# Which up-projection chunks of a ConvFFN go by seven products, and how their low parts are made

## The chip, the cores and the metric

The kernel runs on one core of a Trainium2 chip. The metric is the device time of the core in microseconds, the median of a few executions. An execution's trace tells, engine by engine, what ran when. The engines are TensorE (PE, with its weight loads shown apart as PEld), VectorE (DVE), ScalarE (ACT), GpSimd (POOL) and SyncE (SP); POOL and SP here mostly issue DMAs.

## The reference

Two layers of a decoder trunk over x of 512 tokens by 1024 features: layer 0 with dilated window attention, layer 1 with forgetting attention over shared keys and values, each followed by the same gated ConvFFN. The change touches the up-projection of that ConvFFN alone:

```python
D_MODEL = 1024; SEQ = 512; D_FF = 2816; CONV_W = 3

def conv_ffn(xn, w_up, cw, cb, w_down):
    a = xn @ w_up                                  # 512 x 1024 by 1024 x 5632
    T = a.shape[1]
    ap = jnp.pad(a, ((0, 0), (CONV_W - 1, 0), (0, 0)))
    a = sum(ap[:, j:j + T] * cw[j] for j in range(CONV_W)) + cb
    gate, val = jnp.split(a, 2, axis=-1)
    return (jax.nn.gelu(gate, approximate=True) * val) @ w_down
...
f = conv_ffn(rms_norm(h, g[2]), w_up[l], conv_w[l], conv_b[l], w_down[l])
h = h + rms_norm(f, g[3])
```

## The kernel before

All matrix products are exact to nearly float32 by splitting: each operand is a rounded "high" part (fp32r) plus a "low" part, the rest. A product is three matmuls, high x high, high x low and low x high; `mm3` issues them at L283, L284 and L285, whichever product it is. So every weight tile of 128 x 1024 comes into SBUF (`wraw`, loaded by SP at L50), then its high part is copied by ACT, and its low part is made in one of two ways:

- plainly: DVE subtracts the high part from the raw weight (L78 in `Weights.low`, L683 in `sub_low`);
- by an adding transfer: ACT copies the raw weight with its sign changed to the place of the low part (L71 in `Weights.minus`, L679 in `add_low`), and POOL issues a DMA that adds, so that the place ends as the difference (L98, L680). In the kernel's layout this spares DVE a pass of 128 x 1024 and costs ACT one and POOL a DMA issue.

The up-projection's 5632 columns go by 22 chunks of 128 gate and 128 value columns (`NF` = 22). The loop `for c in range(2, NF)` of `ffn` computes chunks in order; the work of the other engines is written in between by hand, since the kernel runs with a manual schedule: instructions of an engine run in the order in which the code issues them.

A *plain* chunk is two products with all 1024 features and 512 tokens (`up`): 2 x 8 x 3 = 48 matmuls of 512 columns. A chunk in `SEVEN` takes Strassen's scheme in Winograd's form on a 2 x 2 split (features by halves, tokens by halves, the two column groups as the other side): seven products named by their weights A11, S3, S2, A22, A12, S1 and S4, each of 4 x 3 matmuls of 256 columns, 84 in all. The inputs' sums (`XA`, `XB`) are made once per layer, the weights' sums per chunk by DVE (L706, L707, L709, L726), and the outputs' sums by DVE on PSUM (L963 to L1007) with a copy by ACT (L961, or L993 where the chunk was begun early).

The order within a seven chunk c that was begun early is: S2, the taps of chunk c - 1 (the convolution: ACT L620, DVE L621 and L623, then GELU L641), A22, A12, S1; then the beginning of chunk c + 1 (A11 and S3 if it is a seven, with copy L993; half of its first product if it is plain); then S4 of chunk c, and the sums of the outputs (L1001, L1007).

Weights are prepared ahead by two generators that the loop steps through with `next(steps)`: at chunk c they are chained as below, three steps are taken before the beginning of c + 1 when that is a seven, and `run` takes all that is left only under a condition:

```python
steps = chain(steps, weights_b(c + 1), weights_a(c + 2))
...
if c + 1 not in SEVEN or c + 2 in SEVEN:
    run(steps)
```

`weights_a(c)` makes the high and low parts of A11 | A12 (from the raw tile) and S3 | S2 (from the sum `sa`), in two steps; `weights_b(c)` makes S1 | S4 (from `sb`) and A22. For a plain chunk `weights_a` prepares its two tiles, one a step; `ADDED` names the chunks whose first, and whose second tile takes an adding transfer. Before, `SEVEN` has five pairs (4, 5), (7, 8), (10, 11), (13, 14), (16, 17) and the single 19. In a pair the first chunk's lows are added by transfers, the second's are made plainly; the last of them, S1 | S4's, is put off by `late` until after the sum at L1001.

## Time and profile before

| | |
|---|---|
| median of 3 executions | 1109.83 us (1109.48 to 1110.65) |
| the profiled execution | 1109.52 us, span 1107.7 us |
| granted clock of TensorE | 0.998 |
| PE busy | 1098.7 us (99%), 6609 matmuls |
| DVE busy | 876.4 us (79%) |
| ACT busy | 674.2 us (61%) |
| POOL busy | 210.0 us (19%) |
| adding transfers `w<-wsum`, `w<-wraw` | 24 and 32, of 512 KB |

Busy time is the time in which an engine executes; a share under 100% is idle or waiting. The matmuls are pipelined: the distance between the starts of two is shorter than the duration that a row shows. In a row of the timeline stand start, duration, engine, line, operation, tiles (out<-in) and, in brackets, how long the engine had been idle and what ended that. For an issue of a DMA on POOL the duration is that of the issue; when the data have landed is told by the DMA view.

### The profile page before, as it was taken

The page shows a single profiled execution, that of the slowest core. Times are in us where ns is not written, and L with a number is a line of the kernel's source. Part 1 is how long each engine was busy: PE and PEld are TensorE (multiplying, and loading weights), DVE is VectorE, ACT ScalarE, POOL GpSimd, SP SyncE. Part 2 cuts the span into 40 slices and gives each one's busy share as a digit, 9 for nine tenths or more (in the row PEclk, how much of TensorE's full clock was granted, in tenths as well). Part 3 has the DMA queues.
Part 4 walks back from the last instruction along what each step waited for, and adds up shares of the span by engine and source line. Part 5 has one row for each costly group of instructions (what it writes and reads, how often), then busy time and mean ns, then how long its engine had stood idle before and what let it go on. Part 6 is the DMA issues. An engine that isn't in the chain of part 4 may idle for free.

```text
span 1107.7 us, 18081 instructions
## 1 busy us (share of the span) xinstructions
PE 1098.7 (99%) x6609; PEld 951.8 (86%) x6609; DVE 876.4 (79%) x1493; ACT 674.2 (61%) x1116; POOL 210.0 (19%) x309
## 2 busy tenths in 40 slices
PE   9999999999999999999999999999999999999997
PEld 6988889899999988888888788789999999988886
DVE  6697788888778689997685676868887788779894
ACT  7654565755666656576451587746656666747572
POOL 2532001311111211000001445400411111211000
PEclk9999999999999999999999999999999999999999
DMA  9799854467887979793448435594368878989862
GB/s 324 171 381 412 310 161 134 98 181 190 207 199 185 245 263 328 268 333 103 152 134 301 156 96 127 163 285 121 84 178 208 197 186 189 231 266 324 314 247 76
DMA packets 184928, 236.26 MB, mean 213 GB/s; under 512 B 12352, under 2 KB 132152, under 8 KB 184840
## 3 DMA queue, kind: packets, MB, share of 16 engines
q1 hardware_dynamic: 169224, 182.94, 51.0%
q0 software_dynamic: 14944, 52.18, 20.7%
q8 instruction: 52, 0.85, 0.3%
q14 instruction: 36, 0.29, 0.1%
q10 hardware_dynamic: 672, 0.00, 0.0%
HBM read 166.08 MB, written 39.63 MB: 186 GB/s over the span
## 4 chain that ended last, share of the span: by engine, by line
PE 96%; DVE 1%; ACT 1%; issue 1%; POOL 1%; DMA 0%; DVEq 0%; SPq 0%; POOLq 0%; ACTq 0%
PE up L284 13%; PE up L283 13%; PE up L285 13%; PE acc L283 8%; PE acc L284 8%; PE acc L285 8%; PE v_ps L283 2%; PE v_ps L285 2%; PE v_ps L284 2%; PE qk_ps L284 2%; PE qk_ps L283 2%; PE qk_ps L285 2%; PE q_ps L283 1%; PE first L285 1%; PE first L283 1%; PE first L284 1%
## 5 line engine op out<-in xcount | busy, mean ns | idle before, releaser
L283 PE MATMUL acc<-w 128*128 128x512 f32 (+1 forms) x311 | 120.6, 388 | 0.3 <-DVE mix L332 0.3
L285 PE MATMUL acc<-w 128*128 128x512 f32 (+1 forms) x311 | 120.4, 387 | 0.0
L284 PE MATMUL acc<-w 128*128 128x512 f32 (+1 forms) x267 | 103.2, 387 | 0.0
L78 DVE TENSOR_TENSOR w<-wraw,w 128x1024 fp32r<-128x1024 f32 x62 | 82.3, 1347 | 22.9 <-ACT w L60 22.5
L283 PE MATMUL up<-xsh,w 128*128 128x256 f32 x352 | 99.6, 283 | 0.0
L284 PE MATMUL up<-xsl,w 128*128 128x256 f32 x352 | 99.6, 283 | 0.0
L285 PE MATMUL up<-xsh,w 128*128 128x256 f32 x352 | 99.6, 283 | 0.0
L60 ACT CAST w<-wraw 128x1024 fp32r<-128x1024 f32 x82 | 84.7, 1051 | 18.7 <-PE v_ps L284 6.9
L620 ACT ACTIVATE bb<-up,conv 128x512 f32<-128x512 f32 x80 | 59.8, 778 | 58.3 <-DVE up L1007 47.6
L284 PE MATMUL up<-xcl,w 128*128 128x512 f32 (+1 forms) x276 | 93.5, 339 | 0.0
L284 PE MATMUL up<-xbl,w 128*128 128x512 f32 (+1 forms) x276 | 93.5, 339 | 0.0
L283 PE MATMUL up<-xbh,w 128*128 128x512 f32 (+1 forms) x276 | 93.5, 339 | 0.0
L283 PE MATMUL up<-xch,w 128*128 128x512 f32 (+1 forms) x276 | 93.5, 339 | 0.0
L285 PE MATMUL up<-xbh,w 128*128 128x512 f32 (+1 forms) x276 | 93.4, 338 | 0.0
L285 PE MATMUL up<-xch,w 128*128 128x512 f32 (+1 forms) x276 | 93.4, 338 | 0.0
L283 PEld LDWEIGHTS acc<-w 128*128 128x128 f32 x311 | 58.4, 188 | 12.6 <-DVE mix L332 0.7
L285 PEld LDWEIGHTS acc<-w 128*128 128x128 f32 x311 | 58.4, 188 | 11.9
L283 PEld LDWEIGHTS up<-xsh,w 128*128 128x128 f32 x352 | 67.6, 192 | 0.0
L284 PEld LDWEIGHTS up<-xsl,w 128*128 128x128 f32 x352 | 67.6, 192 | 0.0
L285 PEld LDWEIGHTS up<-xsh,w 128*128 128x128 f32 x352 | 67.6, 192 | 0.0
L621 DVE SCALAR_TENSOR_TENSOR bb<-up,conv,bb 128x511 f32<-128x511 f32 x80 | 59.5, 744 | 6.2 <-ACT bb L620 6.1
L623 DVE SCALAR_TENSOR_TENSOR bb<-up,conv,bb 128x510 f32<-128x510 f32 x80 | 59.9, 749 | 2.8
(312 smaller groups left out, 3151.8 us busy)
## 6 DMA issues: line engine op xcount, KB each, us to landing
wraw<-in_w_up_dram SPq DMA_DIRECT2D x88, 512.0 KB, 5.4
w<-wraw POOLq DMA_DIRECT2D x32, 512.0 KB, 6.4
dT<-dsums SPq DMA_DIRECT2D x28, 512.0 KB, 7.0
w<-wsum POOLq DMA_DIRECT2D x24, 512.0 KB, 5.7
dsums<-in_w_down_dram SPq DMA_DIRECT2D x22, 512.0 KB, 7.6
dsums<-in_w_down_dram SPq DMA_DIRECT2D x44, 256.0 KB, 7.8
hD<-hc POOLq DMA_DIRECT2D x44, 256.0 KB, 6.9
dact<-hD SPq DMA_DIRECT2D x44, 256.0 KB, 5.6
```

Source lines behind the costliest of these rows:

```text
L60: self.nc.scalar.copy(pair[:, 0], raw)
L78: self.nc.vector.tensor_tensor(pair[:, 1], raw, pair[:, 0].bitcast(F32), ALU.subtract)
L283: pe.matmul(o, ah, bh, start=first, stop=False, skip_group_check=shared)
L284: pe.matmul(o, ah, bl, start=False, stop=False, skip_group_check=shared)
L285: pe.matmul(o, al, bh, start=False, stop=last, skip_group_check=shared)
L620: act.activation(bb[:, s, :], ps, AF.Identity, bias=cp[:, 3, ch:ch + 1], scale=cp[:, 2, ch:ch + 1])
L621: dve.scalar_tensor_tensor(bb[:, s, 1:], ps[:, :T - 1], cp[:, 1, ch:ch + 1], bb[:, s, 1:], ALU.mult, ALU.add)
L623: dve.scalar_tensor_tensor(bb[:, s, 2:], ps[:, :T - 2], cp[:, 0, ch:ch + 1], bb[:, s, 2:], ALU.mult, ALU.add)
```

## The change

`SEVEN` becomes four runs of three chunks, (4, 5, 6), (8, 9, 10), (12, 13, 14) and (16, 17, 18): 12 of 22 per layer in the place of 11. The plain chunks from 2 on are then 2, 3, 7, 11, 15, 19, 20 and 21. Which seven chunks get plain lows is no longer "the one behind another seven" but a list, `PLAIN_LOWS`: the middle ones 5, 9, 13 and 17. The first and the third of a run have their lows added by transfers. `ADDED` is moved to the plain chunks that are left. Since a third chunk puts nothing into `late`, the loop asks whether there is something in it. Line numbers in the changed kernel are one higher from there on, two higher behind the loop's `late`.

```diff
-SEVEN = 4, 5, 7, 8, 10, 11, 13, 14, 16, 17, 19
-
-ADDED = (6, 9, 12, 15, 18), (18, 20)
+SEVEN = 4, 5, 6, 8, 9, 10, 12, 13, 14, 16, 17, 18
+PLAIN_LOWS = 5, 9, 13, 17
+
+ADDED = (7, 11, 15, 19), (19, 20)
...
             act.copy(w[0][:, 0], r0)
-            if c - 1 not in SEVEN:
+            if c not in PLAIN_LOWS:
                 add_low(w[0], r0)
...
             dve.tensor_tensor(sa[:, 512:1024], sb[:, 0:512], a11, ALU.subtract)
-            if c - 1 not in SEVEN:
+            if c not in PLAIN_LOWS:
                 act.copy(w[1][:, 0], sa)
                 add_low(w[1], sa)
...
             (w0, w1), r0, a12, a22, sa, sb = rest.pop(c)
-            if c - 1 in SEVEN:
+            if c in PLAIN_LOWS:
                 act.copy(w1[:, 0], sa)
                 sub_low(w0, r0)
...
             act.copy(w[1][:, 0, 0:512], a22)
-            if c - 1 in SEVEN:
+            if c in PLAIN_LOWS:
                 sub_low(w1, sa)
             yield
             act.copy(w[0][:, 0], sb)
-            if c - 1 in SEVEN:
+            if c in PLAIN_LOWS:
                 late.append(lambda: sub_low(w[0], sb))
             else:
                 add_low(w[0], sb)
...
                 if c + 1 in SEVEN:
-                    late.pop()()
+                    if late:
+                        late.pop()()
                     dve.tensor_tensor(begun[2], b3, begun[1], ALU.add)
```

In the run 4, 5, 6 the third chunk's `weights_a(6)` is chained at chunk 4, behind `weights_b(5)`: its first step is the third one taken there, and its second step falls to `run` at the end of chunk 4. `weights_b(6)` and `weights_a(7)` follow at chunk 5. The two layers hold 24 chunks of seven products instead of 22.

## The prediction

> **What bounds the kernel now.** I read the page first: the slices of the span, then the chain that ended last.

> ```profile
> span 1107.7 us, 18081 instructions
> PE   9999999999999999999999999999999999999997
> PE 96%; DVE 1%; ACT 1%; issue 1%; POOL 1%; DMA 0%; DVEq 0%; SPq 0%; POOLq 0%; ACTq 0%
> ```

> TensorE (PE) is full in every slice and carries 96% of the chain. Next came the list of what PE waited for, here its two longest entries after the warm-up, and the busy time of the stage that the change touches, the first layer's up-projections (226 to 411 us):

> ```profile
> PE qk_ps L283 <- ACT w L64: 0.4, 1, 0.4
> PE pT_ps L1664 <- DVE prob L1652: 0.4, 1, 0.4
> ...
> 226.00:411.00 185.00, 185.00 (x1245) 171.71 (x1244) 146.60 (x228) 114.30 (x146) 30.60 (x43) 1.00 0.83 207
> ```

> The columns after the stretch are its length and the busy time of PE, weight loads, DVE, ACT and POOL. No wait on an `up` tile is listed, and PE is busy 185.00 of 185 us: today's preparation of weights is hidden altogether. DVE has 38 us free, ACT 71. So fewer matmuls shorten the time directly, and every new wait of PE lengthens it directly. The profiled execution took 1109.52 us, 0.31 below the median of 1109.83; I add differences to the median.

> **What PE saves.** The timeline of PE, and two rows of the same ACT copy one period apart (two chunks by seven products and a plain one):

> ```profile
> 268.12 0.28 PE L283 MATMUL up<-xsh,w 128*128 128x256 f32 x1
> 268.24 0.28 PE L284 MATMUL up<-xsl,w 128*128 128x256 f32 x1
> ...
> 278.06 0.40 PE L283 MATMUL up<-xbh,w 128*128 128x512 f32 x1
> 278.29 0.40 PE L284 MATMUL up<-xbl,w 128*128 128x512 f32 x1
> ...
> 265.44 0.37 ACT L993 COPY csum<-up 128x256 f32<-128x256 f32 x1 [0.22 <-PE up L285]
> 296.52 0.37 ACT L993 COPY csum<-up 128x256 f32<-128x256 f32 x1 [0.22 <-PE up L285]
> ```

> 256 columns take 0.12 us, so a seven chunk (7 x 4 x 3 = 84 matmuls) takes 10.08 us. The period is 31.08 us, which leaves 10.92 for a plain chunk (48 matmuls of 512 columns, 0.2275 each). The change makes one more chunk of each layer a seven (12 for 11): 2 x 0.84 = 1.7 us saved. [...] A difference under 0.2% (2.2 us) can't be told from none, so the saving alone would pass as no change.

> **Where the third chunk's weights come from.** In a run 4, 5, 6 the part `weights_a(6)` is prepared during chunk 4, its second half at the very end: the sum at L709 stands behind L1007, which needs chunk 4's last matmul. Before, a chunk whose lows are added by transfer always had a whole chunk between preparation and use. I follow the new chain from the start of chunk 5's first matmul (t = 0; in the rows 268.12), with distances between rows of before:

> ```profile
> 268.32 0.43 DVE L1007 TENSOR_TENSOR up<-up,csum 128x256 f32<-128x256 f32 x1 [0.94 <-PE up L285]
> 268.66 0.68 DVE L638 TENSOR_TENSOR hc<-bb 128x512 f32<-128x512 f32 x1
> ...
> 275.65 0.68 DVE L709 TENSOR_TENSOR wsum<-wsum,wraw 128x512 f32<-128x512 f32 x1
> ...
> 276.43 1.05 ACT L711 CAST w<-wsum 128x1024 fp32r<-128x1024 f32 x1 [2.17 <-DVE wsum L709]
> 277.38 1.05 ACT L679 ACTIVATE w<-wsum 128x1024 fp32r<-128x1024 f32 x1
> 278.73 1.46 ACT L620 ACTIVATE bb<-up,conv 128x512 f32<-128x512 f32 x2 [0.29 <-DVE up L1007]
> ...
> 278.73 0.86 POOL L680 DMA_DIRECT2D w<-wsum  x1 [3.33 <-DVE up L1007]
> ...
> w<-wsum POOLq DMA_DIRECT2D x24, 512.0 KB, 5.7
> ...
> w<-wsum POOLq DMA_DIRECT2D x1, 512.0 KB, 5.0
> ```

> L1007 starts at 0.20; the instruction behind it 0.34 later, so L709 at 0.54; L711 0.78 later, 1.32; the sign copy L679 0.95 later, 2.27; the adding transfer is issued 1.35 later, 3.62, and lands 5.7 later (median of 24), 9.3. PE wants this low part at the third matmul of chunk 6's S3, begun inside chunk 5 behind S2, A22, A12, S1 and A11: 60 x 0.12 + 0.24 = 7.44. **First wait: 1.9 us.** Bounds of the landing are 5.0 and 6.4 (the issue at 285.46, the last row, and the page's median for transfers from `wraw`, below): 1.2 to 2.6.

> A second chain holds PE nearly as long, so a quicker landing helps little. The same two ACT copies now stand ahead of chunk 4's taps (L620), and so push everything behind them:

> ```profile
> 279.55 0.75 DVE L621 SCALAR_TENSOR_TENSOR bb<-up,conv,bb 128x511 f32<-128x511 f32 x1 [0.26 <-ACT bb L620]
> 282.44 0.68 DVE L726 TENSOR_TENSOR wsum<-wraw,wsum 128x512 f32<-128x512 f32 x1
> ...
> 283.16 1.06 ACT L731 CAST w<-wsum 128x1024 fp32r<-128x1024 f32 x1 [1.35 <-DVE wsum L726]
> 284.12 1.05 ACT L679 ACTIVATE w<-wsum 128x1024 fp32r<-128x1024 f32 x1
> ...
> 263.22 1.05 ACT L60 CAST w<-wraw 128x1024 fp32r<-128x1024 f32 x1
> 264.16 1.06 ACT L71 ACTIVATE w<-wraw 128x1024 fp32r<-128x1024 f32 x1
> ```

> L620 follows L679 by 0.95: 3.22. L621 0.82 later, 4.04; L726 2.89 later, 6.93; L731 0.72 later, 7.65. Then ACT has, 0.95 apart, L679 (8.61, new here: chunk 6's S1 is low-added), L60 (9.56), L71 (10.5), and only then the copy L993 of chunk 6's first product (11.45, 0.37 long). In the built order chunk 6's first S2 matmul waits for that copy: 11.8 against 10.08 on PE, a wait of 1.75 if the first has not already cost it. The two overlap, so together 1.9; lower end 1.75.

> **The plain chunk behind the run.** L71 is the sign copy for chunk 7's first weight, whose low part L98 adds. Its landings, page first, then single issues at 265.5, 296.6, 358.8 and, L680's own, 274.6 us; min, median and maximum of all of POOL's transfers into `w`:

> ```profile
> w<-wraw POOLq DMA_DIRECT2D x32, 512.0 KB, 6.4
> ...
> w<-wraw POOLq DMA_DIRECT2D x1, 512.0 KB, 7.8
> ...
> w<-wraw POOLq DMA_DIRECT2D x1, 512.0 KB, 7.5
> ...
> w<-wraw POOLq DMA_DIRECT2D x1, 512.0 KB, 8.4
> ...
> w<-wraw POOLq DMA_DIRECT2D x1, 512.0 KB, 8.1
> ...
> DMA to landing us min/median/max: 4.5/6.1/8.8
> ...
> 265.51 0.85 POOL L98 DMA_DIRECT2D w<-wraw  x1 [9.70 <-ACT w L71]
> ...
> 274.35 0.39 PE L285 MATMUL up<-xbh,w 128*128 128x512 f32 x1
> ...
> 293.37 2.09 SPq L50 DMA_DIRECT2D wraw<-in_w_up_dram  x3
> ```

> Before, 8.84 us lay between this issue (265.51) and the matmul that needs it (274.35), and 7.5 to 8.4 of them were used: three loads of 512 KB are issued just ahead of it (last row). Now the issue comes at 10.5 + 1.35 = 11.85. Chunk 6 starts at 10.08 + 1.9 = 11.98, its four products take 48 x 0.12 = 5.76, and the low part is wanted at the third 512-column matmul, 0.46 later: 18.2. The window has shrunk to 6.35. At 7.8 us, the middle of three landings in the same place with the same loads ahead, plus now another adding transfer, **the second wait is 1.45 us**; 6.4 gives nothing, 8.4 gives 2.05.

> **What else moves, at nothing.**

> ```profile
> 262.26 1.05 ACT L731 CAST w<-wsum 128x1024 fp32r<-128x1024 f32 x1 [2.42 <-DVE wsum L726]
> ```

> The third chunk's first low part (A11) is issued 8.6 us ahead of its use (L731 stands 4.22 into a first chunk, 262.26 less 258.04; then L703 0.96, L679 0.94 and POOL 1.35 later by the distances above: 7.47 into chunk 4; wanted at 10.08 + 5.76 + 0.24 = 16.08); the 6.4 of the page fits, 8.1 still would. S1's low part is issued at 8.61 + 1.35 = 9.96 and wanted at 11.98 + 4.56 = 16.54; the `wsum` median of 5.7 fits, only because PE is already 1.9 late; without that it would wait about 1. The middle chunk keeps its lows on DVE, in the place they had. ACT gains five sign copies per layer (30 adding transfers for 25) and about three other copies, some 9 us of 71 free; DVE gains at most 6 of 38 free; POOL five issues at 0.86, and only its hidden writes of `hD` queue behind them. SP's loads keep their number.

> **Sum.** Four runs in each of two layers: 8 x (1.9 + 1.45) = 26.8, less 1.7: +25.1, that is 1134.9 us.

> **The rivals.**
> - Only the first wait: the stall lets the loads run dry, L98 lands within 6.4 like the page's median. 8 x 1.9 - 1.7 = +13.5, 1123.3 us. For it: half of all `wraw` transfers are that quick. Against: all of those in this place took 7.5 or more. Chance 0.2.
> - Transfers are quick altogether: landing in under 3.8 us (7.44 - 3.62) would end both waits on them; the copy L993 alone would hold PE 1.75: 8 x 1.75 - 1.7 = +12.3, 1122.1 us. Against it: 5.0 above, and 4.5 for the quickest of all. Chance 0.04. [...]
> - The transfers crowd each other: seven adding transfers in four chunks, for four in three, stretch L98 to 8.8, the slowest of all before. PE without waits reaches its use at 16.3, so both waits together are 11.85 + 8.8 - 16.3 = 4.35: 8 x 4.35 - 1.7 = +33, 1143 us. Chance 0.13.
> - No wait at all, because L709 gets ahead of L1007 or the lead is longer than I read from the order: -1.7, 1108.1 us, no measurable change. It decides from a chain under 7.44 where I count 9.3. Chance 0.05.
> - Faster: no waits, and the 256-column matmuls of the longer runs come at 0.11 instead of 0.12, as the second below does, the first after a stretch of 512 columns:

> ```profile
> 276.63 0.28 PE L283 MATMUL up<-xbh,w 128*128 128x256 f32 x1
> 276.74 0.28 PE L284 MATMUL up<-xbl,w 128*128 128x256 f32 x1
> ```

>   Over the 24 x 84 matmuls of both layers that is 20 us off, besides the 1.7: 1088 us. It decides only if both waits are hidden; the 0.12 holds all through today's runs. Chance 0.02.

> **How the numbers follow.** The forecast has 0.56. It gives 1134.9; the range reaches down to the two rivals with the one wait (1122) and up past the crowded case (1146), leaving out the 0.07 without waits and some tail. Slower by over 0.2%: 0.56 + 0.2 + 0.04 + 0.13 = 0.93; within: 0.05; faster: 0.02.

> **What would show it.** In the profile after, PE's waits should list L285 (its number there is L286) on `up` eight times near 1.9 us with a DMA from `wsum` as releaser, and eight near 1.45 released by a DMA from `wraw`; L711 should stand behind L1007 at the first chunk's end; the up-projection stage should be about 12.5 us longer per layer and all other stages alike. Eight waits only, or L98 landing in 6.4, speaks for the first rival. No gap of PE on `up` makes the forecast wrong.

## The result, and the profile after

The changed kernel takes 1152.9 us (median, 1150.9 to 1154.3), the kernel before 1109.7: a ratio of 1.0386 (95% interval 1.0374 to 1.0399), 43 us more. I had forecast 1134.9 and a range to 1146. The profiled execution took 1154.33 us.

The page of the kernel after, in the same lines as before, with the granted clock:

```profile
span 1152.2 us, 18336 instructions
PE   9999999989898899999999999999999889899997
PEclk9999999998999999999999999999999999999999
PE 81%; DMA 7%; DVE 4%; ACT 4%; issue 2%; POOL 1%; SPq 0%; DVEq 0%; ACTq 0%; POOLq 0%
```

PE was full throughout; now it has gaps in the two up-projection stages, the chain leaves it for DMA, DVE and ACT there, and its clock dips. The first layer's up-projections now end at 435 us instead of 411, the stage of each layer being 22.8 and 19.8 us longer where I had forecast 12.5; the other stages are alike within 0.5 us, but for 1.4 us ahead of the first up-projection. What PE waited for (total, times, longest), and 203 us of the first stage:

```profile
PE up L286 <- DMA w<-wsum: 21.9, 14, 2.9
PE up L286 <- DMA w<-wraw: 6.9, 8, 1.6
PE up L284 <- ACT csum L994: 2.7, 5, 0.7
...
226.00:429.00 203.00, 186.01 (x1265) 171.21 (x1264) 145.39 (x233) 119.87 (x153) 33.97 (x47) 0.98 0.81 197
```

None of these three waits was there before. The first run, 4-5-6, shows all of them. ACT, DVE, POOL and PE, from the timeline; chunk 5's first matmul is at 238.45:

```profile
238.65 0.43 DVE L1009 TENSOR_TENSOR up<-up,csum 128x256 f32<-128x256 f32 x1 [0.87 <-PE up L286]
238.99 0.68 DVE L710 TENSOR_TENSOR wsum<-wsum,wraw 128x512 f32<-128x512 f32 x1
...
239.70 1.06 ACT L712 CAST w<-wsum 128x1024 fp32r<-128x1024 f32 x1 [3.57 <-DVE wsum L710]
240.66 1.06 ACT L680 ACTIVATE w<-wsum 128x1024 fp32r<-128x1024 f32 x1
241.62 1.43 ACT L621 ACTIVATE bb<-up,conv 128x512 f32<-128x512 f32 x2
...
242.01 0.88 POOL L681 DMA_DIRECT2D w<-wsum  x1 [5.27 <-ACT w L680]
...
249.88 0.35 ACT L994 COPY csum<-up 128x256 f32<-128x256 f32 x1
...
247.21 0.39 PE L286 MATMUL up<-xsh,w 128*128 128x256 f32 x1 [1.16 <-DMA w<-wsum]
250.28 0.39 PE L284 MATMUL up<-xsh,w 128*128 128x256 f32 x1 [0.18 <-ACT csum L994]
257.67 0.38 PE L286 MATMUL up<-xsh,w 128*128 128x256 f32 x1 [2.57 <-DMA w<-wsum]
260.64 0.79 PE L286 MATMUL up<-xbh,w 128*128 128x512 f32 x1 [0.60 <-DMA w<-wraw]
```

The four PE rows are S3's low part, the copy of the first product, S1's low part and the plain chunk's low part. The first two are the first wait and its second chain. The third is a wait that I had put at nothing. Its transfer is L681's at 248.37, and L99's follows at 250.50; the loads, the issues and their landings, and then the queues from 248 to 252 us and from 253 to 257 (packets, MB, share of 16 engines):

```profile
246.07 2.14 SPq L51 DMA_DIRECT2D wraw<-in_w_up_dram  x3
...
248.37 0.85 POOL L681 DMA_DIRECT2D w<-wsum  x1 [4.90 <-ACT w L680]
250.50 0.85 POOL L99 DMA_DIRECT2D w<-wraw  x1 [1.29 <-ACT csum L994]
...
w<-wsum POOLq DMA_DIRECT2D x1, 512.0 KB, 9.3
w<-wraw POOLq DMA_DIRECT2D x1, 512.0 KB, 10.1
...
q1 hardware_dynamic: 1848, 0.93, 85.3%
...
q0 software_dynamic: 196, 0.75, 94.2%
q1 hardware_dynamic: 372, 0.18, 16.0%
```

SP's three loads (queue q1) have the engines to themselves until 252; not one packet of POOL's queue q0 moves in those four microseconds. S1's transfer lands 9.3 us after its issue instead of 5.7, L99's, queued behind it, after 10.1. Over the eight runs S1's took 5.9 to 9.3 us and L99's 8.7 to 10.8. From 1.2 us behind the end of the stall on S1 the clock is halved for 6.8 us, 17 matmuls instead of some 30 (columns as in the stage's row, the clock third from the end):

```profile
258.90:265.70 6.80, 6.20 (x17) 4.52 (x17) 1.41 (x4) 2.00 (x2) 1.43 (x2) 0.50 0.94 210
```

Over both layers, taking the distance between the starts of two matmuls less the usual 0.12 or 0.23 us: 15.3 us of waits on S3 and the copy, 12.3 on S1 (in six of the eight runs), 8.5 on L99, 2.6 for matmuls right behind a stall that came 0.1 late, 5.3 for matmuls at half clock, less 1.7 for the saved work. That is 42.3 of the 44.5 us between the two spans; of the other 2.2, 1.4 lie ahead of the first up-projection and 0.5 behind the last, outside the change.

### The profile page after: what moved, and what is told of

It reads as the page before. It is cut to its first block, busy times and chain, and to the rows that moved or that the text cites. A ratio compares the mean times of both kernels' runs of the same rounds, so it can differ in the third digit from the quotient of the medians.

```text
span 1152.2 us, 18336 instructions
## 1 busy us (share of the span) xinstructions
PE 1111.1 (96%) x6681; PEld 959.8 (83%) x6681; DVE 875.7 (76%) x1505; ACT 685.2 (59%) x1132; POOL 218.8 (19%) x319
## 4 chain that ended last, share of the span: by engine, by line
PE 81%; DMA 7%; DVE 4%; ACT 4%; issue 2%; POOL 1%; SPq 0%; DVEq 0%; ACTq 0%; POOLq 0%
PE up L286 9%; PE up L284 8%; PE up L285 8%; PE acc L284 8%; PE acc L285 8%; PE acc L286 8%; DMA w<-wraw 7%; PE v_ps L284 2%; PE v_ps L286 2%; PE v_ps L285 2%; PE qk_ps L285 2%; PE qk_ps L284 2%; PE qk_ps L286 2%; ACT w L680 1%; PE q_ps L284 1%
## 5 line engine op out<-in xcount | busy, mean ns | idle before, releaser
L286 PE MATMUL up<-xsh,w 128*128 128x256 f32 x384 | 110.9, 289 | 21.9 <-DMA w<-wsum 21.9
L284 PE MATMUL acc<-w 128*128 128x512 f32 (+1 forms) x311 | 120.6, 388 | 0.3 <-DVE mix L333 0.3
L286 PE MATMUL acc<-w 128*128 128x512 f32 (+1 forms) x311 | 120.4, 387 | 0.0
L284 PE MATMUL up<-xsh,w 128*128 128x256 f32 x384 | 109.7, 286 | 2.7 <-ACT csum L994 2.7
L285 PE MATMUL up<-xsl,w 128*128 128x256 f32 x384 | 109.1, 284 | 0.0
L285 PE MATMUL acc<-w 128*128 128x512 f32 (+1 forms) x267 | 103.2, 387 | 0.0
L621 ACT ACTIVATE bb<-up,conv 128x512 f32<-128x512 f32 x80 | 59.3, 774 | 67.5 <-DVE up L1009 39.7
L286 PE MATMUL up<-xch,w 128*128 128x256 f32 (+1 forms) x272 | 91.7, 337 | 3.8 <-DMA w<-wraw 3.8
L286 PE MATMUL up<-xbh,w 128*128 128x256 f32 (+1 forms) x272 | 92.1, 339 | 3.0 <-DMA w<-wraw 3.0
L286 PEld LDWEIGHTS up<-xsh,w 128*128 128x128 f32 x384 | 74.2, 193 | 24.8 <-DMA w<-wsum 24.8
L79 DVE TENSOR_TENSOR w<-wraw,w 128x1024 fp32r<-128x1024 f32 x60 | 79.5, 1348 | 17.6 <-ACT w L61 17.1
L284 PE MATMUL up<-xbh,w 128*128 128x256 f32 (+1 forms) x272 | 91.8, 337 | 0.0
L285 PE MATMUL up<-xbl,w 128*128 128x256 f32 (+1 forms) x272 | 91.7, 337 | 0.0
L284 PE MATMUL up<-xch,w 128*128 128x256 f32 (+1 forms) x272 | 91.4, 336 | 0.0
L61 ACT CAST w<-wraw 128x1024 fp32r<-128x1024 f32 x78 | 80.2, 1048 | 18.8 <-DMA wraw<-in_w_up_dram 7.1
L285 PE MATMUL up<-xcl,w 128*128 128x256 f32 (+1 forms) x272 | 91.4, 336 | 0.0
L284 PEld LDWEIGHTS up<-xsh,w 128*128 128x128 f32 x384 | 74.2, 193 | 3.7 <-ACT csum L994 3.7
L285 PEld LDWEIGHTS up<-xsl,w 128*128 128x128 f32 x384 | 74.2, 193 | 0.0
L284 PEld LDWEIGHTS acc<-w 128*128 128x128 f32 x311 | 58.4, 188 | 12.6 <-DVE mix L333 0.7
L286 PEld LDWEIGHTS acc<-w 128*128 128x128 f32 x311 | 58.4, 188 | 11.9
## 6 DMA issues: line engine op xcount, KB each, us to landing
wraw<-in_w_up_dram SPq DMA_DIRECT2D x88, 512.0 KB, 6.7
w<-wraw POOLq DMA_DIRECT2D x34, 512.0 KB, 7.1
w<-wsum POOLq DMA_DIRECT2D x32, 512.0 KB, 5.7
dT<-dsums SPq DMA_DIRECT2D x28, 512.0 KB, 6.6
dsums<-in_w_down_dram SPq DMA_DIRECT2D x22, 512.0 KB, 7.6
```

The lines of the kernel that those rows point to most:

```text
L61: self.nc.scalar.copy(pair[:, 0], raw)
L79: self.nc.vector.tensor_tensor(pair[:, 1], raw, pair[:, 0].bitcast(F32), ALU.subtract)
L284: pe.matmul(o, ah, bh, start=first, stop=False, skip_group_check=shared)
L285: pe.matmul(o, ah, bl, start=False, stop=False, skip_group_check=shared)
L286: pe.matmul(o, al, bh, start=False, stop=last, skip_group_check=shared)
L621: act.activation(bb[:, s, :], ps, AF.Identity, bias=cp[:, 3, ch:ch + 1], scale=cp[:, 2, ch:ch + 1])
```

## The experiments

Two theories stood at the start. A: each of three weight parts is prepared with too short a lead, and the adding transfers land behind the loads. B: the engines or the queues have too much work in a run of three, whatever the order. Ratios are to the kernel before, run on the same chip.

**x1, S1's low part of the third chunk on DVE.**

```diff
+THIRD = 6, 10, 14, 18
...
-            if c in PLAIN_LOWS:
+            if c in PLAIN_LOWS or c in THIRD:
                 late.append(lambda: sub_low(w[0], sb))
```

> The third chunk's S1 and S4 weights get their low part by a DVE subtraction put off by `late`, as the middle chunk's do; nothing else is changed. Theory A (the adding transfer of S1 is served only after the three loads issued just ahead of it, and the next adding transfer L99 queues behind it): the waits of PE on S1, 12.3 us in all over the eight runs, are gone, and L99 lands about 2 us earlier, so that 5 us of wait are left there: about 1137 us. Theory B (the transfers only follow ACT, which has one copy too many in the stretch; L99 lands when the loads let it): PE waits at L99 for what it no longer waits at S1, only the 0.95 us of one ACT copy are won per run: about 1146 us.

Measured: 1128.5 us, ratio 1.0169 (1.0151 to 1.0186), 24 us less than the change. PE's waits, and the landing of the plain chunk's transfer in the first run:

```profile
PE up L287 <- DMA w<-wsum: 9.2, 8, 2.2
PE up L287 <- DMA w<-wraw: 3.8, 4, 1.8
...
w<-wraw POOLq DMA_DIRECT2D x1, 512.0 KB, 6.5
```

Only S3's eight waits are left on `wsum`, and L99's counterpart lands in 6.5 us instead of 10.1 (over the eight runs 6.5 to 8.3 instead of 8.7 to 10.8): the S1 transfer had held it up. That is A's mechanism, larger than I had sized it, partly because the half-speed stretches went down from 13.6 to 3.4 us. The edit also takes one sign copy from ACT, and with it the five waits on the copy L994, 2.7 us, left the list.

**x2, the sum L710 of the third chunk earlier.**

```diff
                 if c + 1 in SEVEN:
+                    if c + 2 in SEVEN:
+                        next(steps, None)
                     if late:
```

> In the first chunk of a run one more preparation step is taken before the put-off subtraction, so that the sum L710 of the third chunk no longer stands behind the output sum that needs the chunk's last matmul; about 2.8 us earlier by the trace. No work is added or left out. Theory A: the first wait (1.92 us per run, S3's low part and the copy of the first product together) is gone, 15.3 us; the waits on S1 and L99 stay as they are, since the whole chain of ACT and PE comes earlier by the same: about 1136 us. Theory B (ACT and the transfers have too much work in the stretch, whatever its order): the wait reappears further on, above 1147 us.

Measured: 1137.8 us, ratio 1.0262 (1.0236 to 1.0289).

```profile
PE up L286 <- DMA w<-wsum: 11.0, 8, 1.9
PE up L286 <- DMA w<-wraw: 8.8, 7, 3.0
```

The time is A's. The wait on the copy has left the list, and in the first three runs of layer 0 no wait on S3 remains; the waits on S1 and on the plain chunk's part stay. S3 still waits in three of the eight runs, the fourth of each layer and the first of layer 1, by 0.7 to 1.6 us, 3.6 in all: there its transfer took 7.3 to 8.3 us, elsewhere 4.6 to 6.5. So most of the first wait was a matter of order alone: the same work, one step earlier, is worth 15 us, a little of it by less time at half clock.

**x3, the plain chunk's first low part on DVE.**

```diff
-ADDED = (7, 11, 15, 19), (19, 20)
+ADDED = (), (19, 20)
```

> The first weight of the plain chunk behind each run (7, 11, 15, 19) gets its low part by a DVE subtraction; one sign copy on ACT and one adding transfer fewer per run. Theory A: the 8.5 us of waits on L99 go, those on S3 and S1 stay, and where the copy of the first product was late ACT wins 0.95 us that the S3 transfer gives back: about 1144 us. Theory B (ACT's copies are what counts): the copy and the S1 chain come 0.95 us earlier per run, 8 x 1.9 = 15 us less with L99's own wait: about 1137 us.

Measured: 1150.4 us, ratio 1.0366 (1.0351 to 1.0382), neither theory's number. PE's waits, DVE's queue in the first run, and the stretch behind it:

```profile
PE up L284 <- DVE up L988: 16.4, 8, 2.6
PE up L286 <- DMA w<-wsum: 8.9, 8, 2.4
...
247.92 1.23 DVE L79 TENSOR_TENSOR w<-wraw,w 128x1024 fp32r<-128x1024 f32 x1 [2.45 <-ACT w L61]
249.06 0.43 DVE L988 TENSOR_TENSOR up<-up,csum 128x256 f32<-128x256 f32 x1
...
249.50:252.90 3.40, 3.35 (x15) 3.36 (x16) 1.14 (x4) 0.00 (x0) 0.00 (x0) 0.50 1.11 284
```

The waits on L99 are gone, and those on S1 too, since PE now comes later to it: the eight on `wsum` are S3's. In their place the new subtraction L79 stood at the head of DVE's queue, waited 2.45 us for the late ACT copy L61, and kept back the output sum L988, which PE's S4 needs. A queue in order made a new wait out of an instruction that nobody was in a hurry for. Each of the eight runs also had a stretch at half clock, behind a stall of 2.0 to 2.7 us, six times this one and twice S3's; together they cost 13 us.

**x4, the three edits together.**

> The three edits of x1, x2 and x3 together. Theory A: no wait on a weight is left, the PE saving of 1.7 us shows: about 1108 us, at most 1114 if DVE, which gains three subtractions of 1.2 us per run, comes late at the output sums. Theory B: DVE then becomes the bound of the run (its added 3.7 us per run against some 5 us free per chunk of four): 1115 to 1125 us.

Measured: 1114.8 us, ratio 1.0045 (1.0030 to 1.0060).

```profile
PE up L287 <- DMA w<-wsum: 2.6, 3, 1.2
PE up L285 <- DVE up L989: 2.4, 5, 0.5
```

Of 43 us 38 are gone, and no clock drop is left in the stage. It lies just above A's bound: S3 still waits in three runs, and the sum behind the subtraction is 0.6 us late in most.

**x5, x1 and x2 without x3.**

> The edits of x1 and x2 together (S1's low part of the third chunk by DVE, and its sum L710 one step earlier), with the adding transfers of the plain chunks as the change has them. Theory A (three separate lead times were too short, and each of the two edits restores one; L100 follows 2 us earlier with them): no wait on `up` in the first three runs of a layer, at most 1.4 us in the fourth, where writes and loads for the down-projection share the queues, so 1.7 us of saving against 2 x 1.4: about 1109 us, between 1107.5 and 1112. Theory B (two chunks with added lows in three are too many transfers, whatever the order): L100 still lands 1 us late in every run, about 1117 us.

Measured: 1116.9 us, ratio 1.0065 (1.0052 to 1.0077).

```profile
PE up L287 <- DMA w<-wraw: 3.8, 3, 2.1
PE up L287 <- DMA w<-wsum: 2.3, 3, 1.1
```

The number is B's, but the wait is not in every run: three runs wait on the plain chunk's transfer, by 0.8 to 2.3 us, the others by nothing or 0.2. These edits leave that transfer a lead of 7.2 to 7.4 us in the three runs, 7.4 to 8.8 elsewhere, and it took 7.2 to 9.7, so the lead is met or missed from run to run. S3 waits as it did in x2, in three runs.

**x6, one load fewer just ahead of S1's transfer.**

```diff
+        W.ahead_dma = 1
         for c in range(2, NF):
...
+            if c == NF - 5:
+                W.ahead_dma = 2
```

> The changed kernel with raw weights loaded one tile less ahead inside the loop (from chunk 2 to 16): by the built order two loads, not three, are then issued just ahead of S1's adding transfer, the third comes 7 us earlier. Nothing else is changed. Theory A (the adding transfers are served behind the loads ahead of them, 512 KB at some 300 KB/us): S1's and L99's transfers land 1.7 us sooner, the first wait stays: 8 x 1.7 = 13.6 less, and fewer drops of the clock, about 1137 us. Theory B (adding transfers take 8 to 10 us there by themselves): S1 still lands 8 us or more after its issue, 1150 us or more. If the raw tiles themselves come late, waits on `wraw` loads appear on ACT and the run decides nothing.

Measured: 1144.1 us, ratio 1.0307 (1.0293 to 1.0321), 9 us less than the change, between the two theories. In the first run:

```profile
w<-wsum POOLq DMA_DIRECT2D x1, 512.0 KB, 7.3
```

S1's transfer lands 2.0 us sooner than the 9.3 above, where A said 1.7. PE's waits on `wsum` in the list are still 12 in number, but told apart by the matmul that waited, in distances between starts, S1's went down from 12.3 to 5.4 us, while S3's and the copy's stayed at 15.5 and L99's at 8.2. So nothing but the place of the loads moved, and of the waits only S1's was cut, by more than half. That loads ahead delay S1's transfer is shown; that they are all of its delay is not.

**x7, all lows of the third chunk on DVE, as the second's.**

```diff
-PLAIN_LOWS = 5, 9, 13, 17
+PLAIN_LOWS = 5, 6, 9, 10, 13, 14, 17, 18
```

> Runs of three with the lows of the second and the third chunk plain, by DVE; no adding transfer is left for a third chunk. Theory A (the transfers' landing and the ACT copies ahead of the taps were the cost, DVE has room): the first wait and the wait on S1 are gone; DVE comes some 0.3 us late at A11's and S3's low part once a run each, 8 x 0.6 = 5: about 1113 us. Theory B (DVE can't carry two plain chunks in a row, 2 x 12.9 us against 2 x 10.1 of PE): its lateness grows over the run and PE waits 2 to 4 us per run, 1125 to 1140 us.

Measured: 1125.4 us, ratio 1.0148 (1.0133 to 1.0164). The only wait on `up` in the list is

```profile
PE up L286 <- DMA w<-wraw: 6.7, 7, 1.6
```

which is the plain chunk's transfer again. B's number, then, but A's mechanism: a lateness of DVE that grows over the run does not show. In every run PE waits twice for the subtraction L684, at A11's and at S3's low part, and each wait costs 0.3 us with the late matmul behind it: 5.1 us in all, the 5 of A. The rest is L99's wait, 8.2 us by the distance of starts, which I had left out of this expectation.

**x8, x4 with the plain chunk's subtraction as a step of its own,** behind the sums that S4 waits for:

```diff
                         W.high()
+                        if i == 0 and c - 1 in THIRD:
+                            yield
                         W.low()
...
                     dve.tensor_tensor(begun[2], b3, begun[1], ALU.add)
+                    if c + 1 in THIRD:
+                        next(steps, None)
```

> x4 with the plain chunk's first low part (7, 11, 15, 19) taken as a step of its own, behind the output sums that S4 waits for, instead of ahead of them. Theory A (the lead of each weight part and the order on DVE are all that was wrong): the 0.63 us that PE waited for DVE's L989 in each run is gone; what stays is S3 in each layer's fourth run, 1.1 to 1.4 us: about 1110.5 us, 1109 to 1112. Theory B (DVE has too much work in a run of three): the 0.6 us reappears at another sum, 1114 us or more.

Measured: 1112.3 us, ratio 1.0018 (1.0009 to 1.0027). The waits on DVE are gone, S3's stay:

```profile
PE up L287 <- DMA w<-wsum: 2.2, 3, 1.2
```

The place of one subtraction in DVE's queue, five waits of 0.6 us, was worth 2.4 us. S3's lead is now 6.6 us; its transfer took 5.7 to 6.5 us in five runs and 7.3 to 7.9 in the three that wait.

**x9, three runs, a pair and a single** (`ADDED` is (18,), (18, 20), and `THIRD` 6, 10, 14).

```diff
-SEVEN = 4, 5, 6, 8, 9, 10, 12, 13, 14, 16, 17, 18
+SEVEN = 4, 5, 6, 8, 9, 10, 12, 13, 14, 16, 17, 19
```

> x8 with three runs of three, one pair and the single 19 (4-5-6, 8-9-10, 12-13-14, 16-17, 19): again twelve chunks by seven products per layer, with the tail as it was before the change. Theory A: no wait on `up` at all, so that the twelfth chunk's saving shows by itself: 1109.8 - 1.7 = 1108.1 us, 1107.5 to 1109. Theory B (a run of three costs something even without a wait, by the order of 256 and 512 columns or by the load on DVE): 1110 us or more.

Measured: 1115.3 us, ratio 1.0044 (1.0030 to 1.0058). A missed: there are still three waits of 1.0 to 2.3 us on `wsum`. Only one of them is S3's, in the first run of layer 1, with a clock drop behind it: the lead is 6.6 us, and this transfer took 8.9 where the other five took 5.7 to 6.7. The other two are not in a run of three at all: they are S1's of the single 19, one in each layer. In layer 0 its transfer, issued at 378.12 us, met loads for the down-projection issued from 377.34 to 378.26 and took 9.2 us; in the kernel before, the first of these loads came 1.4 us behind the transfer, which took 6.0. So two of the three waits of x8 went with the fourth runs, S3's short lead is met in five of six runs, and the tail was not as before after all. What a run of three costs without a wait, x9 does not show.

**x10, x8 with S3's low part on DVE too.**

```diff
                 act.copy(w[1][:, 0], sa)
-                add_low(w[1], sa)
+                if c in THIRD:
+                    yield
+                    sub_low(w[1], sa)
+                else:
+                    add_low(w[1], sa)
```

> x8 with S3's and S2's low part of the third chunk also by DVE, behind the first chunk's last output sum, so that only the third chunk's first tile still takes an adding transfer. Theory A: the last waits (0.65 to 1.3 us on S3, two to three in all) go, and the twelfth chunk's saving shows: 1108.1 us if the rest is as before, 1107.5 to 1109.5. Theory B (DVE, with 3.7 us more per run than in the change as given, is now late at the taps): new waits of PE on DVE or on the copy of the first product, 1111 us or more.

Measured: 1108.4 us (1107.9 to 1108.9) against 1109.9, ratio 0.9984 (0.9975 to 0.9994). No wait on `up` is left, and the stage (226 to 411 us) is PE's alone again:

```profile
PE warm L245 <- DVE zero L240: 1.2, 1, 1.2
PE qk_ps L285 <- ACT w L66: 0.4, 1, 0.4
...
226.00:411.00 185.00, 185.00 (x1284) 173.51 (x1284) 161.56 (x248) 109.80 (x143) 24.72 (x36) 1.00 0.75 190
```

DVE is busy 161.6 of 185 us (146.6 before) and still hides everything: B falls for DVE. For the transfers it stays open in part: x2, x6 and x8 show what order and loads ahead cost, but every kernel that lost the waits on L99 or on S1 altogether also has fewer adding transfers or came later to them. This version beats both kernels, by 1.5 us over the one before: what the twelfth chunk by seven products was worth from the start. The gain is small, but all 11 executions lie below all 15 of the kernel before.

## Why the prediction was right or wrong

- **PE's saving of 1.7 us**: right. x10, without waits, is 1.7 us shorter in the span (1106.0 for 1107.7), 0.88 in each layer's stage for the 0.84 forecast, and 1.5 in the medians.
- **The first wait, 1.9 us per run**: the mechanism right, the size in part by luck. It came to 15.3 us over eight runs, 1.91 each, but five runs took 1.64 to 1.66, below my lower end of 1.75, and the other three 1.9, 2.1 and 3.1. In the first run the chain came as the rows of before had it: L710 at 0.54, L712 at 1.25 for 1.32, L680 at 2.21 for 2.27, the issue at 3.56 for 3.62, the copy L994 at 11.43 for 11.45, S2 at 11.83 for 11.8. The transfer landed a little sooner than 5.7, and the copy then held PE for the rest, so that the second chain set the wait there, not the transfer. x2 confirms the cause.
- **S1's low part at nothing**: this step failed. The issue time was right (9.92 for 9.96), the duration was not: I took the median of 5.7 us where the transfer stands behind the very three loads by which I argued for L98 a paragraph earlier. It took 9.3 in the first run, and the waits came to 12.3 us. x6 shows the loads' part in it, x1 what it cost, with what hung on it.
- **The second wait, 1.45 per run, on L99**: mis-sized. I added "plus now another adding transfer" in words and kept the 7.8 of before. The landing was 10.1 us in the first run. That the wait itself was smaller than forecast, 8.5 us for 11.6, is no merit: PE had already lost time on S1, which gave L99 a longer lead, 9.1 us in the first run for my 6.35. S1 and L99 together cost 2.6 us per run, 20.8 in all, for 11.6 forecast.
- **The clock was left out** of the sum: 5.3 us of matmuls at half clock, and 2.6 of late restarts. I had no term for either. Of the 18 us by which the forecast was short, S1 makes 12.3, these two 7.9, and L99 takes off 3.1.
- **The rivals**: the crowded transfers (1143 us, 0.13) came nearest in size, 4.35 us per run for 4.5 measured, and x1 bears it out for L99; S1's delay came in good part from the loads (x6), and it lacked the clock. Its price should have been the likeliest, since three transfers and three loads were to meet in the order that I had in hand.
- **DVE's and ACT's room**: the sums of busy time held (x10: DVE 161.6 and ACT 109.8 of 185 us), but x3 shows that they say nothing about a queue whose head waits, there 2.45 us.

## What to carry to other kernels

Where an engine is full, every piece prepared beside it has a lead (from the last input to the first use) and a chain; work out both for each piece that is moved, and take a transfer's duration from a row with the same transfers ahead of it, never from the median of all (here 9.3 us for a median of 5.7). When a step is prepared one chunk later than its neighbours were, look first whether it stands behind an instruction that waits for the bound engine: moving it in front may cost nothing (x2: 15 us less). A subtraction on an engine with room can be cheaper than a transfer with none, if it stands behind what others wait for: a ratio of 1.0018 in x8, against 1.0065 with the transfer in x5 and 1.0045 with the subtraction ahead in x4.

## What the runs showed of the hardware that I had not expected

The length of a stall alone does not tell: in the trace of the change the stall of 1.73 us that ends at 994.91 has a stretch behind it, the one of 2.28 that ends at 352.61 has none. What goes with the stretches is where a stall lies. In that trace the three start at 258.91, 948.40 and 996.19 us, 202 and 14 steps of 3.413 us apart; in x3 at 249.49, 297.28, 341.65 and 389.44 us, 14, 13 and 14 such steps, and so on to the eighth. Four windows on this grid, from the trace of the change (length, PE busy, weight loads, DVE, ACT, POOL, the clock third from the end):

```profile
907.44:910.86 3.42, 1.75 (x15) 1.55 (x14) 3.09 (x5) 2.52 (x3) 0.33 (x1) 1.00 1.07 213
910.86:914.27 3.41, 2.88 (x18) 2.21 (x17) 2.28 (x5) 1.16 (x2) 0.52 (x1) 1.00 1.04 289
992.77:996.19 3.42, 1.69 (x14) 1.48 (x13) 1.73 (x4) 2.99 (x4) 0.69 (x1) 1.00 0.92 245
996.19:999.60 3.41, 3.41 (x18) 3.41 (x17) 1.01 (x3) 1.28 (x3) 1.59 (x3) 0.50 0.92 232
```

With 1.67 us of PE idle in the first window the next one keeps its clock; with 1.73 in the third the next one is at half. Over the six traces that have such stretches, each of the 18 follows a window at full clock in which PE was idle for 1.73 to 2.85 us, and no such window without a stretch behind it held more than 1.73. The stall of 2.28 us lay across a boundary of this grid: PE was idle for 0.75 us in the window from 347.66 and for 1.54 in the one from 351.07, and the clock stayed at 1.00. This is what these traces show; why the clock does so, and where the line runs in another kernel, they do not.

The other surprise is the order in the queues: while SP's loads kept the 16 engines busy at 85.3%, POOL's queue moved nothing for four microseconds (248 to 252 us above). S1's first packet came 4.0 us behind its issue, where that of the adding transfer at 235.86 us, with no load under way, came after 1.45. It is no strict order, though: from 259 to 261 us both queues moved packets, at 67% and 44% of the engines.
